# An output projection by seven products of halves, with its weight sums and some attention work made ready early through DRAM

## The chip, the cores and the metric

The kernel runs on one core of a Trainium2 chip. The metric is the time of one launch on the device in microseconds (us), as the median of several runs. The engines named below are TensorE (PE in the profile; PEld is its loading of weights), VectorE (DVE), ScalarE (ACT), GpSimd (POOL) and SyncE (SP), whose queue carries nearly all transfers between DRAM and the on-chip memory.

## The reference

One layer of a hybrid encoder on 1024 prompt frames and 32 single-frame samples, all in float32, D_MODEL = 1024:

```python
h = rmsnorm(x, g_mix)
proj = h @ w_in
q, k, v, cb, cc, cx, ga, gc = jnp.split(proj, SPLITS, axis=-1)
...
y_attn = attend(q, k, v).reshape(b, t, SB_WIDTH) @ w_attn_out
conv_out, new_buf = causal_conv(cc * cx, conv_buf, conv_w)
y_conv = (cb * conv_out) @ w_conv_out
merged = jax.nn.sigmoid(ga) * y_attn + jax.nn.sigmoid(gc) * y_conv
x = x + merged @ w_o
f = jnp.square(jax.nn.relu(rmsnorm(x, g_ffn) @ w_up)) @ w_down
x = x + f
x = x + jax.nn.sigmoid(rmsnorm(x, g_ple) @ w_ple_gate) * (p @ w_ple)
```

`attend` is a strictly causal stick-breaking attention with 8 heads of 64. The change concerns `merged @ w_o`, a product of 1024 x 1024 weights with 1056 columns, and the work that feeds `merged`.

## The kernel before, in words

All 1056 columns (prompt and samples) are handled at once, features on the 128 partitions, so a 1024-feature matrix is 8 blocks of 128 x 1056. Each float32 operand is split into a high part (rounded to the fp32r form by a cast on ACT, `whi`, `mh`) and a low part (the rest, a subtraction on DVE, `wlo`, `ml`); each product is three matmuls: high x high, high weight x low, low weight x high.

The stages follow each other on PE: the first gate groups, the input projection in 18 column sets, the start of the attention, the attention, the two branch projections (`branches`), the output projection (`output_projection`), the MLP's up and down projections, and the gated embedding. The input, up and down projections already use seven products of halves instead of eight (`seven`): with the weights in quadrants A11, A12, A21, A22 and the columns in halves, sums S1 to S4 of weight quadrants and T1 to T4 of operand quadrants are formed, and the products A11·B11, A12·B21, A22·T4, S1·T1, S2·T2, S3·T3, S4·B22 give the result.

The output projection before is the plain product: `wo_group` makes, for each of 8 output blocks and each third of the columns (352), 8 x 3 matmuls; `wo_post` adds the group to x in DRAM order, `wo_high` and `wo_low` split the weights one block ahead, `wo_after` squares the new x and makes the MLP's operands of it, `wo_sums` their T1 to T4, which go out to DRAM and come back for `up_early`, the first products of the MLP.

What sets the order: on PE, ACT, DVE and POOL the instructions run in the order in which the program text issues them (`tc.manual_schedule`), each engine in order, and an instruction that has to wait holds all that stand behind it on its engine. Small generators in the list `side` are stepped once per group of matmuls and so lay the preparation of the next weights between the groups; in the attention a planned list of filler matmuls (`plan_gates`, `plan_rest`) stands between the steps. The transfers stand on SP's queue in one order, which a scheduler fixed when the kernel was built; a transfer that waits for its data holds those behind it too. Buffers come in rings: 34 blocks of 128 x 1056 (`blk`), 4 raw weight blocks, and 2 buffers each for the split weights `whi` and `wlo`. A new tile waits until the last reader of the one that had the buffer is done.

The gate rows (16 blocks of 128 x 1056, eight for the attention branch, numbers 0 to 7, and eight for the convolution, 8 to 15) are made in the input projection, kept in DRAM (`gd`), and read again in `branch_fetch`; `branch_scale` and `branch_sigmoid` finish them on DVE and ACT before `branch_post` multiplies.

## Time and profile before

| what | value |
|---|---|
| time of the runs shown | median 1539.77 us (1539.54 to 1540.97, 3 runs) |
| the profiled execution | 1540.83 us, with a span of 1539.1 us |
| granted TensorE clock in it | 0.998 |
| PE busy over the span | 1517.4 us (99%) |
| DVE, ACT, POOL busy | 1082.9, 751.3, 294.9 us |
| input projection in the span | 63.6 to 391 us |
| start and body of the attention | 391 to 401.6 and 401.6 to 602.6 us |
| branch projections | 602.6 to 672.8 us |
| output projection | 672.8 to 766.1 us |
| first products of the MLP (`up_early`) | 766.1 to 791.5 us |
| down projection | 1098 to 1426.2 us |

The bounds of the stages were read from the first and last matmul of each stage's groups. Tables by stretch give, for each stretch, its length and each engine's busy time with its count of instructions in brackets. A group of instructions is given by its line in the kernel, its engine, the names of output and inputs without buffer numbers, and the shape; matmuls of one stream overlap, so that the distance between their starts, not the mean duration, is their cost. In a list of waits, "A <- B" is an instruction A that waited for B. Of a stretch in time order, each row has the start, the duration and, in brackets, the engine's idle time before it and what ended it.

### The profile page before, as it was taken

What the parts mean: (1) busy time and instruction counts of PE and PEld (TensorE: products, weight loads), DVE (VectorE), ACT (ScalarE), POOL (GpSimd) and SP (SyncE); (2) the same over time, 40 slices, a digit from 0 to 9 for tenths busy, and PEclk for the clock granted to TensorE, in tenths of its full rate; (3) what the DMA queues carried; (4) which work ended last, traced back from release to release, by engine and by line L of the source; (5) the groups of instructions that cost most, each with busy time, mean ns of one, the idle gap of its engine ahead of it and who ended that gap; (6) DMA issues with size and microseconds to landing.
All of it is one profiled execution on the core that took longest, in us unless ns stands there. A gap on an engine that the chain in (4) does not pass through costs nothing.

```text
span 1539.1 us, 29455 instructions
## 1 busy us (share of the span) xinstructions
PE 1517.4 (99%) x11792; PEld 1505.0 (98%) x11792; DVE 1082.9 (70%) x1483; ACT 751.3 (49%) x1378; POOL 294.9 (19%) x324
## 2 busy tenths in 40 slices
...
GB/s 217 205 52 114 192 153 193 167 43 129 240 126 242 223 124 123 147 167 182 128 199 171 160 175 169 149 138 154 304 283 200 280 334 236 203 274 121 138 129 117
DMA packets 112009, 273.21 MB, mean 178 GB/s; under 512 B 13152, under 2 KB 30304, under 8 KB 111872
## 3 DMA queue, kind: packets, MB, share of 16 engines
...
q14 instruction: 45, 0.37, 0.1%
...
## 4 chain that ended last, share of the span: by engine, by line
PE 62%; ACT 1%; DVE 1%; DMA 0%; issue 0%; DVEq 0%
PE ps_dn L1759 7%; PE ps_dn L1758 7%; PE ps_dn L1757 7%; PE ps_A11u L242 3%; PE ps_A11u L241 3%; PE ps_A11u L240 3%; PE ps_pg L118 2%; PE ps_S1u L241 2%; PE ps_S1u L240 2%; PE ps_wo L1433 2%; PE ps_wo L1432 2%; PE ps_wo L1431 2%; PE ps_S1u L242 2%; PE ps_pg L120 2%; PE ps_pg L119 2%; PE ps_oa L118 1%
## 5 line engine op out<-in xcount | busy, mean ns | idle before, releaser
L1759 PE MATMUL ps_dn<-fh,wlo_dn 128*128 128x264 f32 x896 | 255.2, 285 | 0.0
L1758 PE MATMUL ps_dn<-fl,whi_dn 128*128 128x264 f32 x896 | 254.9, 284 | 0.0
L1757 PE MATMUL ps_dn<-fh,whi_dn 128*128 128x264 f32 x896 | 254.7, 284 | 0.0
L1759 PEld LDWEIGHTS ps_dn<-fh,wlo_dn 128*128 128x128 f32 x896 | 168.6, 188 | 0.1
L1757 PEld LDWEIGHTS ps_dn<-fh,whi_dn 128*128 128x128 f32 x896 | 168.7, 188 | 0.0
L1758 PEld LDWEIGHTS ps_dn<-fl,whi_dn 128*128 128x128 f32 x896 | 168.5, 188 | 0.0
L207 POOL TENSOR_TENSOR s_i<-raw_i,raw_i 128x512 f32<-128x512 f32 x32 | 44.2, 1381 | 240.0 <-DVE slS_i L168 209.9
L852 DVE TENSOR_TENSOR_SCAN r<-r 128x128 f32<-128x128 f32 (+3 forms) x64 | 86.4, 1349 | 3.4 <-POOL r L845 3.4
L1644 ACT CAST whi_dn<-raw_dn 128x1024 fp32r<-128x1024 f32 x40 | 42.0, 1050 | 82.8 <-PE ps_dn L1758 82.6
L1650 DVE TENSOR_TENSOR wlo_dn<-raw_dn,whi_dn 128x1024 fp32r<-128x1024 f32 x40 | 61.2, 1530 | 28.6 <-ACT whi_dn L1644 28.6
L240 PE MATMUL ps_A11i<-T,shS_i 128*128 128x264 f32 x256 | 73.1, 285 | 0.0
L242 PE MATMUL ps_A11i<-T,slS_i 128*128 128x264 f32 x256 | 72.9, 285 | 0.0
L241 PE MATMUL ps_A11i<-T,shS_i 128*128 128x264 f32 x256 | 72.7, 284 | 0.0
L207 POOL TENSOR_TENSOR s_u<-raw_u,raw_u 128x512 f32<-128x512 f32 x22 | 32.1, 1459 | 210.3 <-DVE slS_u L168 126.8
L892 DVE TENSOR_TENSOR at<-pa,at 128x512 fp32r<-128x512 f32 (+2 forms) x96 | 51.9, 550 | 26.6 <-ACT at L891 22.1
L1670 DVE TENSOR_TENSOR fl<-mr,fh 128x1056 fp32r<-128x1056 f32 x56 | 69.9, 1247 | 0.2 <-ACT q L1710 0.2
L168 DVE TENSOR_TENSOR slS_i<-s_i,shS_i 128x512 fp32r<-128x512 f32 x48 | 35.0, 734 | 49.6 <-ACT shS_i L166 49.4
L1519 ACT ACTIVATE m<-m 128x528 f32<-128x528 f32 (+1 forms) x52 | 31.7, 610 | 73.2 <-DVE m L287 28.3
L845 POOL TENSOR_SCALAR_AFFINE_SELECT r<-r 128x128 f32<-128x128 f32 x64 | 30.5, 477 | 187.1 <-ACT r L838 175.8
L1841 POOL TENSOR_TENSOR xx<-xx,pgs 128x384 f32<-128x384 f32 (+1 forms) x23 | 24.3, 1058 | 217.0 <-DVE pgs L1840 210.4
L1433 PE MATMUL ps_wo<-mh,wlo_wo 128*128 128x352 f32 x192 | 62.1, 324 | 0.0
L1432 PE MATMUL ps_wo<-ml,whi_wo 128*128 128x352 f32 x192 | 62.1, 323 | 0.0
...
## 6 DMA issues: line engine op xcount, KB each, us to landing
raw_dn<-in_w_down_dram SPq DMA_DIRECT2D x56, 512.0 KB, 4.6
raw_i<-in_w_in_dram SPq DMA_DIRECT2D x36, 512.0 KB, 4.5
mr<-mdT SPq DMA_DIRECT2D x32, 528.0 KB, 5.6
raw_u<-in_w_up_dram SPq DMA_DIRECT2D x32, 512.0 KB, 3.6
mr<-mdB SPq DMA_DIRECT2D x24, 528.0 KB, 6.0
...
raw_pg<-in_w_ple_gate_dram SPq DMA_DIRECT2D x17, 512.0 KB, 3.5
...
```

What stands on the lines that cost most here:

```text
L207: f()
L240: nc.tensor.matmul(p_, wh[:, k, :], o[:, 0, c], start=new and n == 0, stop=False, **on)
L241: nc.tensor.matmul(p_, wh[:, k, :], o[:, 1, c], start=False, stop=False, **on)
L242: nc.tensor.matmul(p_, wl[:, k, :], o[:, 0, c], start=False, stop=z, **on)
L852: nc.vector.tensor_tensor_scan(rev, rev, rev, 1.0, ALU.mult, ALU.bypass)
L1432: nc.tensor.matmul(ps, hi[:, k, :], ml[k][:, c], start=False, stop=False, skip_group_check=True)
L1433: nc.tensor.matmul(ps, lo[:, k, :], mh[k][:, c], start=False, stop=k == KD - 1, skip_group_check=True)
L1650: dve(lo, raw, hi.bitcast(F32), op=sub)
L1670: dve(l, mraw.pop(v), opd[v].bitcast(F32), op=sub)
L1757: nc.tensor.matmul(ps, hi[:, j, :], oh, start=j == 0, stop=False)
L1758: nc.tensor.matmul(ps, hi[:, j, :], ol, start=False, stop=False)
L1759: nc.tensor.matmul(ps, lo[:, j, :], oh, start=False, stop=j == NP_ - 1)
```

## The change

`w_o` is multiplied by seven products. The 28 products of 128 output rows (4 row pairs j, 7 kinds) each run over two quarters of 264 columns, 4 blocks of weights and 3 matmuls, 672 matmuls of 264 columns in place of 576 of 352: first the four A12·B21, then per row pair A11, A22 (of the pair before), S1, S2, S4, S3, and last A22 of pair 3. Each product is added to x, held in quadrants, as soon as it is done (`dve` lines in `output_projection`), and each quadrant goes to DRAM by itself.

The weight sums S1 to S4 are made in 16 pieces (`ahead_wo`) while the input projection's sets 6 onward run, split into high and low, and kept in DRAM (`wsd`); 8 pieces split `w_attn_out` in the same way (`ahead_attn`, kept in `aod`) in the first 48 steps of the attention, and four gate rows, 4 to 7, are scaled and put through the sigmoid (`ahead_gate`, kept in `gs_`) in the last two sets of the input projection and the start of the attention. So that these four exist by then, the first two sets compute rows 4 to 7, and rows 0 to 3 are made by the planned filler in place of 4 to 7. In `branches` the attention products read the split weights, and rows 4 to 7 ready to use. The operands B11, B21, B22 and T1 to T4 of the new product (`wop`) are made from `merged` in the branches and in the projection's first groups. The MLP's operands B21 and B22 of row pairs 0 to 2 are made after the projection from x read back from DRAM (`xg`, `xh`), and B11 late in it.

In the diff, lines with "..." stand for what is left out.

```diff
+AHEAD_AT = {6: 14, 16: 14}
...
-    SETS = [("g", 0), ("g", 2)] + [(nm, 0) for nm in ("cc", "cx", "cb", "q", "k", "v")] + [("g", 8)]
+    SETS = [("g", 4), ("g", 6)] + [(nm, 0) for nm in ("cc", "cx", "cb", "q", "k", "v")] + [("g", 8)]
...
+    def ahead_wo(j, k):
+
+        t = blk(f"wr{j}{k}", F32R, [P, 2, 2, 2, P])
+        raw = t[:, 1].bitcast(F32)
+        for i in range(2):
+            nc.sync.dma_start(raw[:, i], w_o[2 * j + i][:, 2 * k : 2 * k + 2, :])
+        for _ in range(3):
+            yield
+        a11, a12, a21, a22 = raw[:, 0, 0], raw[:, 0, 1], raw[:, 1, 0], raw[:, 1, 1]
+        dve(a22, a21, a22, op=add)
+        dve(a21, a11, a21, op=sub)
+        dve(a11, a22, a11, op=sub)
+        dve(a12, a11, a12, op=sub)
+        nc.scalar.copy(t[:, 0], raw)
+        yield
+        dve(t[:, 1], raw, t[:, 0].bitcast(F32), op=sub)
+        nc.sync.dma_start(wsd[j][:, :, :, k, :].rearrange("x s p n -> p (x s) n"), t.bitcast(F32).rearrange("p x r e n -> p (x r e) n"))
+        yield
+
+    def ahead_attn(n):
+        t = blk(f"ao{n}", F32R, [P, 2, 4, P])
+        raw = t[:, 1].bitcast(F32)
+        nc.sync.dma_start(raw, w_attn_out[n])
+        for _ in range(3):
+            yield
+        nc.scalar.copy(t[:, 0], raw)
+        dve(t[:, 1], raw, t[:, 0].bitcast(F32), op=sub)
+        nc.sync.dma_start(aod[n], t.bitcast(F32).rearrange("p e k n -> p e (k n)"))
+        yield
+
+    def ahead_gate(n):
+        m = blk(f"ga{n}")
+        nc.sync.dma_start(m, gd[n])
+        for _ in range(3):
+            yield
+        scaled(m)
+        yield
+        nc.scalar.activation(m, m, AF.Sigmoid)
+        nc.sync.dma_start(gs_[n - 4], m)
+        yield
+
+    AHEAD = [partial(ahead_wo, j, k) for j in range(4) for k in range(4)]
+    AHEAD += [partial(ahead_gate, n) for n in range(4, 8)] + [partial(ahead_attn, n) for n in range(KD)]
+
+    def ahead_some(n):
+        for _ in range(min(n, len(AHEAD))):
+            yield from AHEAD.pop(0)()
...
+            w = wraw.tile([P, 2, 4, P], F32R, tag="raw", name=f"raw_o{nm}{n}")
+            nc.sync.dma_start(w.bitcast(F32).rearrange("p e k n -> p e (k n)"), aod[n])
         sg = blk(f"s{nm}{n}")
-        nc.sync.dma_start(sg, gd[n + (8 if nm == "c" else 0)])
+        nc.sync.dma_start(sg, gd[n + 8] if nm == "c" else gs_[n - 4] if n > 3 else gd[n])
...
+        if nm == "a":
+            made[b] = tuple(fetched[b][0][:, i] for i in range(2))
+            return
...
+    wop = {k: [None] * 4 for k in ("B11", "B21", "B22", "T1", "T2", "T3", "T4")}
+
+    def part_high(k, j, src):
+        d = wop[k][j] = blk(f"o{k}{j}", F32R, [P, 2, TH])
+        nc.scalar.copy(d[:, 0, :], src)
+
+    def part_low(k, j, src):
+        d = wop[k][j]
+        dve(d[:, 1, :], src, d[:, 0, :].bitcast(F32), op=sub)
+        wop[k][j] = d[:, 0, :], d[:, 1, :]
...
+    def merge_sums(n, ks=("T3", "T2", "T4")):
+
+        a, b = halves
+        e, o = mg[n - n % 2], mg[n // 2 * 2 + 1] if n % 2 else None
+        if o is None:
+            dve(e[:, a], e[:, a], e[:, b], op=sub)
+            return
+        for k in ks:
+            if k == "T3":
+                dve(e[:, b], o[:, b], e[:, b], op=sub)
+            elif k == "T2":
+                dve(o[:, b], o[:, b], e[:, a], op=add)
+            else:
+                dve(o[:, a], o[:, a], o[:, b], op=sub)
...
+    def turn_part(k, j):
+
+        n, c = 2 * j + (k in ("T2", "T4")), halves[k in ("T2", "T3")]
+        part_high(k, j, mg[n][:, c])
+        part_low(k, j, mg[n][:, c])
...
+                proj_high("A12", 1)
+                proj_low("A12", 1)
+                proj_fetch("A12", 2)
...
+            elif s_ in AHEAD_AT:
+                prior = ahead_some(AHEAD_AT[s_])
+                side.append(prior)
...
+            if n < 48:
+                next(prior, None)
...
+    PROJ = [("A12", "B21", j) for j in range(4)]
+    for j in range(4):
+        PROJ += [("A11", "B11", j)] + [("A22", "T4", j - 1)] * (j > 0)
+        PROJ += [("S1", "T1", j), ("S2", "T2", j), ("S4", "B22", j), ("S3", "T3", j)]
+    PROJ += [("A22", "T4", 3)]
+    AT = {(k, j): 2 * i for i, (k, _, j) in enumerate(PROJ)}
...
+    def proj_fetch(k, j):
+        if k in PLACE:
+            r, e = PLACE[k]
+            oraw[k, j] = wraw.tile([P, 4, P], F32, tag="raw", name=f"raw_{k}o{j}")
+            nc.sync.dma_start(oraw[k, j], w_o[2 * j + r][:, e::2, :])
+            return
+        ow[k, j] = w = [fpool.tile([P, 4, P], F32R, tag=g, name=f"{g}o{k}{j}", bufs=SHB) for g in ("sh", "sl")]
+        for i in range(2):
+            nc.sync.dma_start(
+                w[i].bitcast(F32).rearrange("p k n -> p (k n)"), wsd[j, i, PART[k]].rearrange("p k n -> p (k n)")
+            )
...
+        for q, k in enumerate(("S1", "S2", "S4", "S3")):
+            at(q, proj_fetch, k, 0)
+        for j in (2, 3):
+            at(2 * j - 3, proj_high, "A12", j)
+            at(2 * j - 2, proj_low, "A12", j)
+        at(2, xload, "ce", 2)
+        at(2, xload, "ce", 3)
+        at(3, xload, "xb", 0)
+        at(3, xload, "m2", 0)
+        at(1, merge_high, last, "2")
+        for q, k, j in (
+            (1, "T1", 0), (2, "T1", 1), (3, "T1", 2), (4, "T1", 3), (6, "T2", 0), (7, "T2", 1), (8, "T2", 2), (9, "T2", 3),
+            (10, "T3", 0), (11, "T3", 1), (12, "T3", 2), (13, "T3", 3), (14, "T4", 0), (15, "T4", 1), (16, "T4", 2), (17, "T4", 3),
+        ):
+            at(q, turn_part, k, j)
+        at(3, merge_low, last, "2")
+        at(4, merge_sums, last, ("T3",))
+        at(5, merge_sums, last, ("T2",))
+        at(6, merge_sums, last, ("T4",))
+        for (k, j), q in AT.items():
+            if k in ("A11", "A22"):
+                at(max(1, q - 9), proj_fetch, k, j)
+                at(q - (3 if (k, j) == ("A11", 0) else 5), proj_high, k, j)
+                at(q - (2 if (k, j) == ("A11", 0) else 4), proj_low, k, j)
+            elif k != "A12" and j:
+                at(q - 6, proj_fetch, k, j)
...
+        def again(j):
+            if j % 2 == 0:
+                x21[0] = blk(f"xg{j}", F32, [P, 2, TH])
+            x21[j + 1] = x21[0][:, j % 2, :]
+            nc.sync.dma_start(x21[j + 1], xd[2 * j + 1][:, halves[0]])
...
+        for j in range(3):
+            at(AT["S4", 3] + 2 + j // 2, again, j)
+        at(end - 12, early_up, 0)
+        at(end - 10, early_up, 1)
+        at(end - 4, early_split, "u0")
+        at(end - 2, early_split, "u1")
+        at(end - 1, second, 0)
...
+            for t in range(2):
+                on = (z if k in ("S1", "S4") else x).get((j, t)) if k not in ("A11", "S1") else None
+                if i < 2:
+                    proj(k, b, j, t, on, range(3, 4), False, True)
+                else:
+                    p_ = proj(k, b, j, t, on)
+                    (z if k in ("S1", "S4") else x)[j, t] = p_
+                for f in jobs.pop(2 * i + t, ()):
+                    f()
...
+                if k in ("A11", "A12"):
+                    dve(x11, p_, x11, op=add)
+                elif k == "S1":
+                    dve(x22, x22, p_, op=sub)
+                elif k == "S2":
+                    dve(x12, p_, x12, op=add)
+                elif k == "S4":
+                    dve(x12, x12, p_, op=sub)
+                elif k == "S3":
+                    dve(x22, p_, x22, op=add)
+                else:
+                    dve(x21_, p_, x21_, op=add)
...
+        up_operand("B21", 3, x1[3][2])
+        keep_x(3, 2)
+        for j in (1, 2):
+            second(j)
+        square_x(3, 2)
+        up_operand("B22", 3, x1[3][3])
+        add_square(last)
...
+                    elif i == 2 and j < 3:
+                        if j % 2 == 0:
+                            pair = blk(f"xh{j}", F32, [P, 2, TH])
+                        x22[j] = pair[:, j % 2, :]
+                        nc.sync.dma_start(x22[j], xd[2 * j + 1][:, halves[1]])```

Three places where instructions now stand otherwise. Each row is one instruction (or several alike, x2) with its line, its operation, output and inputs, and shape; the names are the program's with the index left out, and a number tells buffers apart.

The first is SP's queue at the start of the attention. `q` are the first queries, `ks` and `vv` keys and values, `ga` a gate row, `gs_` its place in DRAM, `m_i` results of the last input set, `cv` cached values. Before:

```order
L808 DMA vv_4855<-vd 128x1024
L820 DMA q_4945<-qd 64x2x256
L821 DMA q_4945<-qd 64x256
L822 DMA q_4945<-qd 64x256
L820 DMA q_4949<-qd 64x2x256
L821 DMA q_4949<-qd 64x256
L822 DMA q_4949<-qd 64x256
L1280 DMA gd<-m_i_4612 128x1056
L1280 DMA gd<-m_i_4613 128x1056
L820 DMA q_4955<-qd 64x2x256
```

and with the change:

```order
L860 DMA vv_5035<-vd 128x1024
L651 DMA ao_5110<-in_w_attn_out_dram 128x512
L872 DMA q_5130<-qd 64x2x256
L873 DMA q_5130<-qd 64x256
L667 DMA gs__158<-ga_5001 128x1056
L874 DMA q_5130<-qd 64x256
L872 DMA q_5134<-qd 64x2x256
L873 DMA q_5134<-qd 64x256
L874 DMA q_5134<-qd 64x256
L1384 DMA gd<-m_i_4778 128x1056
L1384 DMA gd<-m_i_4779 128x1056
L872 DMA q_5140<-qd 64x2x256
```

The last of the four finished gate rows (the last `gs_` row) now stands between the second and the third load of the first `q`; before, the queue went from one `q` load to the next.

The second is ACT at the start of the output projection. `w0oA` is the high part of a weight quadrant (the third and fourth A12, then the first A11), `raw_A` the same as loaded; `oB` and `oT` are operands of the new product, `mg` and `sc` blocks of `merged`. Before, `whi_wo` is the high part of a weight block and `mh` that of `merged`:

```order
L971 ACTIVATE sa_8456<-sa_8456 128x1056
L1417 CAST whi_wo_8572<-raw_wo_8512 128x1024
L991 CAST mh_8589<-mg_8183 128x1056
L991 CAST mh_8610<-mg_8293 128x352 x2
L1417 CAST whi_wo_8635<-raw_wo_8569 128x1024
L991 CAST mh_8610<-mg_8293 128x352
L1417 CAST whi_wo_8725<-raw_wo_8632 128x1024
```

With the change:

```order
L1551 CAST w0oA_8805<-raw_A12o_8763 128x512
L1052 CAST oB_8826<-mg_8506 128x528
L1551 CAST w0oA_8889<-raw_A12o_8809 128x512
L1052 CAST oB_8891<-mg_8506 128x528
L1052 CAST oT_8893<-sc_6064 128x528
L1052 CAST oT_8911<-sc_7001 128x528
L1551 CAST w0oA_8922<-raw_A12o_8874 128x512
L1052 CAST oT_8928<-mg_8192 128x528
L1052 CAST oT_8948<-mg_8395 128x528
L1551 CAST w0oA_8967<-raw_A11o_8896 128x512
```

The casts of the first T operands (`oT` from `sc`) stand behind the cast of the third A12.

The third is DVE at the same place: `w1oA` is the low part of a weight quadrant, `ceo` the x quadrant to which a product in `ps_wo` is added. Before, the low parts of the weights and the three additions of block 0:

```order
L994 TENSOR_TENSOR ml_8611<-mg_8293,mh_8610 128x352
L1423 TENSOR_TENSOR wlo_wo_8707<-raw_wo_8569,whi_wo_8635 128x1024
L1436 TENSOR_TENSOR xr_8511<-ps_wo_0_8638,xr_8511 128x352
L1436 TENSOR_TENSOR xr_8511<-ps_wo_1_8660,xr_8511 128x352
L1436 TENSOR_TENSOR xr_8511<-ps_wo_2_8682,xr_8511 128x352
L1423 TENSOR_TENSOR wlo_wo_8752<-raw_wo_8632,whi_wo_8725 128x1024
```

With the change:

```order
L1693 TENSOR_TENSOR ceo_8786<-ps_woA_8829,ceo_8786 128x264
L1056 TENSOR_TENSOR oT_8893<-sc_6064,oT_8893 128x528
L1693 TENSOR_TENSOR ceo_8786<-ps_woA_8839,ceo_8786 128x264
L1555 TENSOR_TENSOR w1oA_8906<-raw_A12o_8809,w0oA_8889 128x512
L1056 TENSOR_TENSOR oT_8911<-sc_7001,oT_8911 128x528
L1693 TENSOR_TENSOR ceo_8786<-ps_woA_8849,ceo_8786 128x264
L1056 TENSOR_TENSOR oT_8928<-mg_8192,oT_8928 128x528
L1056 TENSOR_TENSOR oB_8891<-mg_8506,oB_8891 128x528
L1693 TENSOR_TENSOR ceo_8786<-ps_woA_8859,ceo_8786 128x264
L1555 TENSOR_TENSOR w1oA_8946<-raw_A12o_8874,w0oA_8922 128x512
L1056 TENSOR_TENSOR oT_8948<-mg_8395,oT_8948 128x528
L1080 TENSOR_TENSOR mg_8395<-mg_8506,mg_8395 128x528
```

Between the additions of the first groups stand the low parts of T1 and of the weights, and the sums that make T3, T2 and T4 of the last pair.

286 lines of the change are left out of this document (172 added, 114 removed).

## The prediction

> **What bounds the kernel now.** The page's head first: PE is busy nearly all of the span, no other engine is.
>
> ```profile
> span 1539.1 us, 29455 instructions
> PE 1517.4 (99%) x11792; PEld 1505.0 (98%) x11792; DVE 1082.9 (70%) x1483; ACT 751.3 (49%) x1378; POOL 294.9 (19%) x324
> ```
>
> So a change pays only through what PE has to do and through what PE waits for. The table by stretch shows where that is: in order the input projection, the start of the attention, the attention, the branches, the output projection, the MLP's first products, and the down projection for comparison.
>
> ```profile
> core 0: us, PE busy (x) PEld busy (x) DVE busy (x) ACT busy (x) POOL busy (x), PEclk, DMA share, GB/s
> 63.60:391.00 327.40, 326.59 (x2669) 325.34 (x2668) 216.17 (x292) 146.33 (x315) 93.73 (x60) 1.00 0.40 138
> 391.00:401.60 10.60, 10.60 (x89) 10.60 (x88) 3.69 (x5) 3.34 (x7) 0.00 (x0) 1.00 0.56 168
> 401.60:602.60 201.00, 198.05 (x1531) 189.91 (x1530) 167.11 (x236) 124.64 (x282) 40.31 (x130) 1.00 0.58 175
> 602.60:672.80 70.20, 69.65 (x434) 69.36 (x434) 55.37 (x75) 26.96 (x32) 0.00 (x0) 1.00 0.48 158
> 672.80:766.10 93.30, 93.30 (x580) 93.30 (x579) 44.38 (x60) 24.81 (x31) 15.24 (x6) 1.00 0.44 158
> 766.10:791.50 25.40, 23.76 (x192) 23.34 (x192) 21.36 (x30) 20.83 (x41) 0.00 (x0) 1.00 0.79 265
> 1098.00:1426.20 328.20, 328.20 (x2691) 328.14 (x2690) 263.53 (x315) 135.78 (x167) 27.62 (x16) 1.00 0.73 244
> ```
>
> The output projection has no idle PE at all, and DVE and ACT are half free in it. The attention is the stretch with the least room on DVE (167 of 201), and `up_early` the one where DVE and ACT are both over 80% busy. The list of PE's waits says the same: of waits in the stretches that the change touches there are only these of any size, two of them in `up_early` (1.6 + 0.7 = 2.3 us).
>
> ```profile
> PE ps_eu L240 <- ACT pe L221: 1.6, 1, 1.6
> PE av L909 <- DVE at L892: 1.2, 2, 0.7
> PE ps_A11u L242 <- DVE wlo_u L110: 0.7, 1, 0.7
> ```
>
> **The gain: fewer matmul columns.** The distance between matmuls is read from the first and the last start of a product's groups, for the plain product (352 columns) and for the down projection, which already has the form that the change brings (264 columns).
>
> ```profile
> L1431 PE MATMUL ps_wo<-mh,whi_wo x192: 318/323/328, 673.0 to 765.6; 128*128 128x352 f32 x192
> L1433 PE MATMUL ps_wo<-mh,wlo_wo x192: 317/323/328, 673.3 to 765.9; 128*128 128x352 f32 x192
> ...
> L1757 PE MATMUL ps_dn<-fh,whi_dn x896: 278/284/291, 1098.1 to 1425.8; 128*128 128x264 f32 x180
> L1759 PE MATMUL ps_dn<-fh,wlo_dn x896: 278/284/373, 1098.4 to 1426.1; 128*128 128x264 f32 x180
> ```
>
> 576 matmuls from 673.0 to 765.9 are 92.9 / 575 = 161.6 ns each (161.9 with the whole stretch, 93.3 / 576); 2688 from 1098.1 to 1426.1 are 328.0 / 2687 = 122.1 ns. So the projection goes from 93.2 us to 672 x 122.1 ns = 82.0 us: **-11.2 us** as long as nothing makes PE wait. The other stages keep their counts of matmuls (the gate rows only change places).
>
> The distance per column is the same in both, 0.46 ns; 39.5 ns more for 88 columns leaves about 3 ns that is fixed. [...]
>
> **The cost at the projection's start.** The new product needs much small preparation in its first groups, in the fixed order of ACT and DVE. Its pieces, by rows of the same shapes:
>
> ```profile
> L168 DVE TENSOR_TENSOR slA_i<-raw_i,shA_i 128x512 fp32r<-128x512 f32 x16 | 11.0, 689 | 20.9 <-ACT shA_i L166 20.9
> L287 DVE TENSOR_TENSOR m_i<-ps_A12i,p_i 128x264 f32<-128x264 f32 x32 | 13.1, 425 | 6.4 <-PE ps_A12i L242 6.4
> L166 ACT CAST shA_i<-raw_i 128x512 fp32r<-128x512 f32 x16 | 10.0, 623 | 0.1
> ```
>
> Back to back they follow each other some 0.1 us faster than they last, as the T operands in `up_early` show (three in 1.94 us on DVE; two ACT starts 0.53 apart):
>
> ```profile
> 774.51 1.94 DVE L162 TENSOR_TENSOR T<-rt,T 128x528 fp32r<-128x528 f32 x3
> ...
> 776.33 0.64 ACT L161 CAST T<-w 128x528 fp32r<-128x528 f32 x1
> 776.86 0.65 ACT L1558 ACTIVATE ce<-ce 128x528 f32<-128x528 f32 x1
> ```
>
> So I take 0.62 us for a 528-column subtraction or sum, 0.60 for a 512-column one, 0.35 for adding a 264-column product, 0.53 and 0.62 for the casts. Count from the first matmul. The first two A12 take three of their four blocks in both quarters, 36 matmuls, then the last block, 3 matmuls a group. The third A12's cast needs the buffer of the first A12 (two buffers), free after 42 matmuls, at 5.15 us. ACT then runs that cast, B22_3 and T1_0: 5.15 + 0.62 + 0.53 + 0.63 = 6.9. DVE has added the first group at about 5.2 and stands at the low part of T1_0 until 6.9; behind it queue that low part, the second group's addition and the low part of the third A12: 6.9 + 0.62 + 0.35 + 0.60 = 8.5. PE's third matmul of the third A12 wants it at 50 x 0.122 = 6.1: a stall of 2.4 us. From there DVE does not rest. Up to the fourth A12's low part it has 3 pieces of 0.62, 2 additions and 0.60: 8.5 + 3.2 = 11.7, wanted 24 matmuls (2.9 us) after 8.5 = 11.4, a stall of 0.2. Up to the first A11's low part it has 5 of 0.62, 2 of 0.35 and 0.60 more: 16.0, wanted at 14.6, a stall of 1.4. After that the parts are ahead of PE: the T2 parts are wanted only six groups later. Sum **+4.0 us**. If DVE's order did not matter, the buffer alone would cost 5.15 + 0.62 + 0.60 = 6.4 against 6.1, 0.3 us; if each of the pieces took its full duration, about 5.5. I take 4.0, since each step is in an order that can't change.
>
> The rest of the projection has transfers for it: half-sized weight sums come back from DRAM in high and low parts.
>
> ```profile
> DMA packets 4818, 14.74 MB, mean 158 GB/s; under 512 B 544, under 2 KB 544, under 8 KB 4813
> ```
>
> That is the projection before. After, S1 to S4 bring 16 x 512 KB = 8.4 MB, a quarter of the 4.2 MB of w_o falls away, x read again adds 0.8 MB: some 22.9 MB in 86 us, 266 GB/s, as much as `up_early` moves now (265). Hidden, taken at 0.
>
> **The cost at the attention's start.** The last finished gate row's store now stands on SP between the loads of the first queries. The rows before, ACT, SP, PE and transfers in turn:
>
> ```profile
> 400.39 0.38 ACT L706 COPY sg<-ps_g 128x264 f32<-128x264 f32 x1 [1.62 <-PE ps_g L704]
> ...
> L621 ACT ACTIVATE m_i<-m_i 128x1056 f32<-128x1056 f32 x6 | 6.6, 1092 | 0.0
> ...
> 395.12 0.60 SPq L821 DMA_DIRECT2D q<-qd  x1
> 395.76 0.59 SPq L822 DMA_DIRECT2D q<-qd  x1
> ...
> 401.70 0.28 PE L835 MATMUL z<-ks,q 128*128 128x128 f32 x1
> ...
> q<-qd SPq DMA_DIRECT2D x3, 128.0 KB, 3.0
> q<-qd SPq DMA_DIRECT2D x5, 64.0 KB, 3.4
> ```
>
> Before, the third load was issued at 395.76, 6 us ahead of the matmul at 401.70 that reads it. With the change it stands behind the store, and the store waits for the row's sigmoid, which stands on ACT behind the second copy of the filler gate (the row at 400.39, tied to PE). The sigmoid starts at 400.7 and ends at 401.8, the store's issue takes 0.6, the load lands 3.4 us after its issue began: 401.8 + 0.6 + 3.4 = 405.8. The second matmul of the first scores needs it, and PE is in order: 405.8 - 401.7 = 4.1. With the 3.0 us of the larger ones it would be 3.7; I take **+3.9**. The next queries' loads stand behind it with 0.6 us each, about as late as their readers: no more. PE has no idle time in that stretch to pay from.
>
> **The smaller terms.** *After the projection*: `up_early` gets five more operand pairs (B21 and B22 of the pairs 0 to 2, less one that falls into the projection), and one weight split less.
>
> ```profile
> L1373 DVE SCALAR_TENSOR_TENSOR B<-xr,vecT,B 128x528 fp32r<-128x528 f32 x12 | 8.8, 761 | 0.0
> L110 DVE TENSOR_TENSOR wlo_u<-raw_u,whi_u 128x1024 fp32r<-128x1024 f32 x12 | 15.2, 1263 | 3.8 <-ACT whi_u L109 2.9 <-DMA raw_u<-in_w_up_dram 0.9
> ```
>
> 5 x 0.76 - 1.26 = 2.5 us more on DVE, which has 25.4 - 21.4 = 4.0 free: between -1.6 (the first wait goes, since both first weights are split earlier) and +2.5. I take +0.6. *Input projection*: 16 pieces with four additions of 128 x 128 columns, a cast and a low part each, some 1.5 us of DVE, 24 us over a stage in which DVE has 111 us free; PE feels it only where one of them waits for a transfer and an addition that PE needs stands behind. 0 to +8 (the rival below); I take +0.5. *Attention*: 8 pieces of 0.60 on DVE and 0.52 on ACT, 4.8 us of the 34 that DVE has free: 0 to +4.8, taken +0.5. *Branches*: DVE loses eight low parts of 512 and four scalings and gains sums and more, smaller parts; 15 us free there, and PE idles 0.5: 0, between -0.5 and +1.
>
> **Sum**: -11.2 + 4.0 + 3.9 + 0.6 + 0.5 + 0.5 = **-1.7 us**. The sum belongs to the profiled execution, 1540.83 us (span 1539.1 and 1.7 around it), which is 1.06 above the median of the runs. Against that median of 1539.77 I predict **1538.1 us**. This kernel's measurement can tell 0.2%, 3.1 us, from no change.
>
> **The rivals.**
> *Only one of the two stalls is there* (a load that lands sooner, an ACT order that the waits treat more kindly): -1.7 - 4 = -5.7, 1534.1 us. For it: each stall is a chain of four or five steps worked out by hand. Against: each engine is in order and the waits are between named instructions.
> *Neither*, PE alone counts: -11.2 + 1 = -10, 1529.6 us. For it: the down projection, same form, has PE busy 328.20 of 328.20 us. Against: that stage's weights are prepared by a long, even stream, not from a standing start.
> *The attention pays its pieces in full*: DVE is its busiest helper, and the pieces go in the steps where scans and the attention weights share it. -0.5 + 4.8 added: +2.6, 1542.4 us. Against: fillers on PE between the steps.
> *Slower*: in the input projection, DVE stands at a piece whose load or store has not landed, with the addition of a product behind it. The nearest rows for such a transfer are:
>
> ```profile
> raw_i<-in_w_in_dram SPq DMA_DIRECT2D x36, 512.0 KB, 4.5
> mr<-mdT SPq DMA_DIRECT2D x32, 528.0 KB, 5.6
> ```
>
> PE goes on without an addition for about three groups of 12 matmuls, 4.4 us; a wait of 5.6 costs 1.2 us. If half of the 16 pieces hit one, +9.6 instead of +0.5: net +7.4, 1547.2 us. It decides from about five such pieces on (net over 3.1). For it: 28 of 34 blocks are in use there, so pieces take turns with the results' blocks. Against: a piece's load is issued three steps ahead.
> *The weight load paces*, 161.9 ns for each matmul however many columns: 108.8 us for the projection, net +25, 1565 us. Only the down projection's rows speak, and against it. [...]
>
> **How the numbers follow.** Forecast 0.55, within it 0.15 of the weight below -3.1 us; one stall 0.17; neither 0.05; attention in full 0.09; slower 0.13; weight load 0.01. Faster by over 0.2% then is 0.15 + 0.17 + 0.05 = 0.37, slower 0.14, no change 0.40 + 0.09 = 0.49. The forecast alone spans 1535 to 1542. The range, 1532 to 1543.5, takes in the one-stall case and the attention case and leaves out the two ends.
>
> **What would show it.** 672 matmuls 122 ns apart from the tenth group on; PE waits of about 2.4, 0.2 and 1.4 us for low parts of A12 and A11 in the first 16 us; one PE wait of about 4 us for a `q` transfer at the first scores; no PE wait over 1 us in the input projection. Wrong it is if the first or second of these stalls is missing (faster), or if the input projection is more than 3 us longer than 327.4 (slower).

## The result and the profile after

The changed kernel takes **1595.51 us** (median of 4 runs, 1594.4 to 1598.03), the kernel before beside it 1539.94 (1539.54 to 1540.97): a ratio of 1.0362, 95% interval 1.0344 to 1.038. It is 3.6% slower; predicted were 1538.1 us and no change.

The head of the profiled execution's page shows that PE has not only waited, it has also been busy for longer (before: 1517.4 us):

```profile
span 1594.9 us, 30094 instructions
PE 1527.8 (96%) x11888; PEld 1508.4 (95%) x11888; DVE 1147.5 (72%) x1633; ACT 762.7 (48%) x1424; POOL 301.4 (19%) x324
```

To see where, both spans are cut at the same matmuls: from the last first-gate product to the end of the input projection's sets (input), to the second matmul of the first scores (z), to the first attention output product (attention), to the first output projection product (branches), to the end of `up_early` (projection and up_early), to the first down product (up), and the rest. The table by stretch of the changed kernel, first five stages (length, each engine's busy time with its count, the granted clock, the DMA share and GB/s):

```profile
core 0: us, PE busy (x) PEld busy (x) DVE busy (x) ACT busy (x) POOL busy (x), PEclk, DMA share, GB/s
57.60:437.40 379.80, 349.43 (x2744) 343.43 (x2742) 260.57 (x378) 158.99 (x343) 95.28 (x60) 0.96 0.48 162
437.40:452.50 15.10, 9.80 (x64) 9.21 (x62) 5.50 (x6) 5.13 (x9) 0.00 (x0) 0.86 0.73 206
452.50:666.40 213.90, 207.20 (x1565) 197.92 (x1566) 175.90 (x250) 131.01 (x293) 45.88 (x130) 0.99 0.66 208
666.40:730.50 64.10, 64.10 (x398) 64.10 (x397) 47.73 (x72) 13.55 (x19) 0.00 (x0) 1.00 0.49 165
730.50:847.00 116.50, 108.66 (x864) 107.10 (x864) 82.68 (x142) 52.60 (x95) 14.82 (x6) 0.99 0.79 263
```

and the same stretches of the kernel before:

```profile
57.50:394.20 336.70, 335.87 (x2743) 334.41 (x2742) 220.96 (x299) 152.58 (x327) 93.73 (x60) 1.00 0.40 140
394.20:401.70 7.50, 7.50 (x64) 7.50 (x63) 1.23 (x1) 2.09 (x4) 0.00 (x0) 1.00 0.49 165
401.70:609.40 207.70, 204.21 (x1568) 195.78 (x1568) 171.85 (x243) 126.87 (x286) 40.31 (x130) 1.00 0.58 177
673.00:791.60 118.60, 116.96 (x769) 116.54 (x769) 65.77 (x91) 45.54 (x72) 15.24 (x6) 1.00 0.52 180
```

Of the 55.8 us that the span grew, the input projection has 43.1 (379.8 - 336.7), the start of the attention 7.6, the attention 6.2, the branches 0.5; the two stages for which the change was made gain 2.1, and the rest is within 0.5. In the input projection PE stood for 30.4 us (379.80 - 349.43; before 0.8), and was busy 13.6 us longer (349.43 - 335.87) with the same matmuls, at a granted clock of 0.96.

The list of PE's waits, in the same order as the page gives them:

```profile
PE ps_A11i L241 <- DVE m_i L295: 17.4, 7, 7.9
PE ps_A11i L241 <- ACT u_i L285: 6.5, 5, 3.6
...
PE ps_woA L1728 <- DVE w1oA L1555: 3.4, 2, 2.2
PE pt_v L572 <- DVE dv L559: 3.4, 1, 3.4
PE z L887 <- DMA q<-qd: 2.9, 1, 2.9
PE ps_eu L243 <- DVE wlo_eu L111: 2.5, 2, 1.7
PE ps_g L754 <- ACT m_i L746: 2.0, 1, 2.0
PE ps_eu L241 <- ACT pe L222: 1.9, 2, 1.7
```

The first, second and fourth rows are the input projection: `m_i` and `u_i` are the additions and copies that empty the products' accumulators, on DVE and ACT. The waits for `w1oA` and `q` were forecast; those for `wlo_eu` and `pe` lie in `up_early`, for which the forecast had +0.6 us in all. What DVE and ACT stood for in that stage:

```profile
DVE m_i L288 <- DMA wsd<-wr: 8.9, 2, 4.7
DVE wr L638 <- DMA wr<-in_w_o_dram: 8.6, 3, 4.1
DVE m_i L295 <- DMA kd<-m_i: 4.4, 1, 4.4
...
ACT wr L642 <- DVE wr L641: 69.3, 13, 15.3
```

`wr` is the block in which a piece of weight sums is made, `wsd` its place in DRAM. DVE waits for the landing of a piece's store (the next result `m_i` takes the block from which it is stored), for the landing of a piece's load, and for the landing of a result's store. ACT's cast of a piece (L642) waits for DVE's sums, and holds the copies behind it. ACT itself stood at two transfers of pieces too, 7.9 us at a load and 4.5 us at a store.

How one such wait grows is seen in the longest of them, in order of time (start, duration, engine, line; in brackets the idle time before and what ended it; SPq are transfers as they are issued):

```profile
181.28 0.69 DVE L644 TENSOR_TENSOR wr<-wr 128x512 fp32r<-128x512 f32 x1
182.00 0.37 SPq L645 DMA_DIRECT2D wsd<-wr  x1
186.17 0.77 DVE L288 TENSOR_TENSOR m_i<-ps_A12i,p_i 128x264 f32<-128x264 f32 x2 [4.20 <-DMA wsd<-wr]
186.86 1.21 DVE L548 TENSOR_TENSOR m_i<-m_i,kh 128x1024 fp32r<-128x1024 f32 x1
188.10 0.81 SPq L634 DMA_DIRECT2D wr<-in_w_o_dram  x2
188.96 5.42 SPq L549 DMA_DIRECT2D kd<-m_i  x2
192.46 0.43 DVE L295 TENSOR_TENSOR m_i<-ps_A11i,s_i 128x264 f32<-128x264 f32 x1 [4.39 <-DMA kd<-m_i]
192.95 0.59 PE L241 MATMUL ps_A11i<-T,shA_i 128*128 128x264 f32 x1 [7.87 <-DVE m_i L295]
```

A piece is stored at 182.00. The next addition needs its block and starts only at 186.17, when the store has landed. Through that the low part of a key block (L548) is late, and its store stands on SP behind the loads of the next piece (188.10). The addition after that needs this block, and waits a second time, 4.39 us. Two waits of 4.3 us in a row leave PE 7.87 us without work.

And then PE starts at half the clock. PEclk, the granted clock, is 1.00 or 0.50 throughout this trace. It is 0.50 (half speed below) from 188.71, 222.84, 267.22 and 407.16 us in the input projection, from 441.30 and 451.54 in the next two stages, from 816.76 in `up_early`, and again from 1588.18 to the end. These starts are 10, 13, 41, 10, 3, 107 and 226 steps of 3.41 us apart, and the stretches before the last are one to three such steps long. The table by stretch, cut into these steps:

```profile
188.71:198.95 10.24, 6.00 (x27) 6.00 (x28) 6.00 (x13) 2.25 (x5) 0.65 (x1) 0.50 0.52 174
222.84:226.25 3.41, 3.09 (x15) 3.12 (x16) 1.95 (x7) 1.56 (x4) 0.00 (x0) 0.50 0.11 45
260.39:263.80 3.41, 1.68 (x14) 1.46 (x12) 2.48 (x6) 1.45 (x2) 0.00 (x0) 1.00 0.00 0
267.22:270.63 3.41, 3.41 (x16) 3.18 (x16) 2.63 (x4) 0.18 (x1) 0.00 (x0) 0.50 1.03 369
274.04:277.46 3.42, 1.73 (x12) 1.52 (x12) 2.93 (x8) 1.73 (x4) 0.00 (x0) 1.00 0.85 303
407.16:417.40 10.24, 6.59 (x28) 6.29 (x29) 7.13 (x15) 1.66 (x3) 0.00 (x0) 0.50 0.48 156
437.88:441.30 3.42, 1.68 (x12) 1.62 (x13) 2.90 (x4) 1.97 (x4) 0.00 (x0) 1.00 1.03 311
441.30:444.71 3.41, 3.41 (x18) 3.41 (x17) 1.26 (x1) 0.53 (x2) 0.00 (x0) 0.50 1.01 229
468.60:472.02 3.42, 1.68 (x14) 1.43 (x13) 1.22 (x2) 1.87 (x4) 0.37 (x1) 1.00 0.77 241
734.84:738.25 3.41, 2.10 (x16) 1.77 (x15) 1.29 (x4) 2.49 (x5) 0.00 (x0) 1.00 0.92 317
738.25:741.67 3.42, 2.49 (x20) 2.49 (x21) 3.42 (x8) 1.32 (x3) 0.00 (x0) 1.00 0.37 117
813.35:816.76 3.41, 1.70 (x13) 1.49 (x13) 3.20 (x3) 0.18 (x1) 1.44 (x1) 1.00 0.49 190
```

From 441.30 to 444.71 PE is busy all the time, and its matmuls start 0.22 us apart, 16 of them from 441.31 to 444.60 (3.29 / 15), where 28 at a distance of 122 ns would fit. The four rows at half speed in the input projection have 86 matmuls (those cut by the ends of a row with them) in 19.09 us of busy PE, 222 ns each. At 122 ns they would take 10.5 us: by this estimate 8.6 of the 13.6 us by which PE was busy longer are half speed, and the other 5.0 are not explained here.

The length of one wait does not tell whether half speed follows. In the steps before 441.30 and 816.76 waits of 1.96 and 1.71 us end, and PE was busy for 1.68 and 1.70 us of these steps. The wait of 2.24 us that ends at 739.18 lies across two steps, with 2.10 and 2.49 us busy, and nothing followed. Counted over this trace, between 60 and 1500 us: half speed came after each of the five full-speed steps with PE busy for 1.51 us or less, after two of the five with 1.68 to 1.73 us (not after those at 260.39, 274.04 and 468.60), and after none of the 399 with 1.92 us or more. What decides among the five is not shown.

### The profile page after: what moved, and what is told of

Same layout as the page of the kernel before. It is cut to its first block, busy times and chain, and to the rows that moved or that the text cites. A ratio compares the mean times of both kernels' runs of the same rounds, so it can differ in the third digit from the quotient of the medians.

```text
span 1594.9 us, 30094 instructions
## 1 busy us (share of the span) xinstructions
PE 1527.8 (96%) x11888; PEld 1508.4 (95%) x11888; DVE 1147.5 (72%) x1633; ACT 762.7 (48%) x1424; POOL 301.4 (19%) x324
## 3 DMA queue, kind: packets, MB, share of 16 engines
q8 instruction: 93, 1.52, 0.4%
## 4 chain that ended last, share of the span: by engine, by line
PE 58%; DVE 2%; ACT 1%; DMA 1%; issue 1%; DVEq 0%; ACTq 0%; SPq 0%
PE ps_dn L2001 7%; PE ps_dn L2002 7%; PE ps_dn L2000 7%; PE ps_A11u L242 3%; PE ps_A11u L243 3%; PE ps_A11u L241 3%; PE ps_woA L1728 3%; PE ps_pg L119 2%; PE ps_S1u L242 2%; PE ps_S1u L241 2%; PE ps_S1u L243 2%; PE ps_pg L120 2%; PE ps_pg L121 2%; PE ps_woS L1728 1%; PE ps_oa L121 1%; PE ps_oa L119 1%
## 5 line engine op out<-in xcount | busy, mean ns | idle before, releaser
L241 PE MATMUL ps_A11i<-T,shS_i 128*128 128x264 f32 x256 | 74.9, 293 | 7.0 <-ACT u_i L285 6.5
L897 POOL TENSOR_SCALAR_AFFINE_SELECT r<-r 128x128 f32<-128x128 f32 x64 | 36.1, 565 | 206.8 <-ACT r L890 195.7
L243 PE MATMUL ps_A11i<-T,slS_i 128*128 128x264 f32 x256 | 73.5, 287 | 0.0
L169 DVE TENSOR_TENSOR slS_i<-s_i,shS_i 128x512 fp32r<-128x512 f32 x48 | 40.9, 857 | 35.0 <-ACT shS_i L167 33.3
L169 DVE TENSOR_TENSOR slS_u<-s_u,shS_u 128x512 fp32r<-128x512 f32 x48 | 35.4, 738 | 35.2 <-ACT shS_u L167 35.2
L1908 ACT CAST fh<-mr 128x1056 fp32r<-128x1056 f32 x56 | 60.0, 1074 | 0.0
```

The costliest lines, as they stand in the source:

```text
L169: dve(l, src, h.bitcast(F32), op=sub)
L241: nc.tensor.matmul(p_, wh[:, k, :], o[:, 0, c], start=new and n == 0, stop=False, **on)
L243: nc.tensor.matmul(p_, wl[:, k, :], o[:, 0, c], start=False, stop=z, **on)
```

## The experiments

Each total is one run unless an interval is given. Stages are cut as above, in us of the profiled execution; the kernel before took 1539.9 to 1543.3 us beside them. The expectations of e1, e3 and e4 count the input projection from a bound 6.0 us later (373.8 us in the change, 330.7 before). In e1, e9 and e11 the projection reads split attention weights in place of the weight sums, and e3 stores values that are not the sums: they time the work, not the result.

| run | total | input | z | attention | branches | projection + `up_early` |
|---|---|---|---|---|---|---|
| before | 1539.94 | 336.7 | 7.5 | 207.7 | 63.6 | 118.6 |
| after | 1595.51 | 379.8 | 15.1 | 213.9 | 64.1 | 116.5 |
| e1_none | 1554.29 | 344.7 | 12.2 | 211.0 | 64.0 | 115.5 |
| e3_nomath | 1570.3 | 357.5 | 12.9 | 213.4 | 63.5 | 116.0 |
| e4_spread | 1610.89 | 395.4 | 13.0 | 214.8 | 64.0 | 115.9 |
| e5_gates | 1592.58 | 376.5 | 11.7 | 217.0 | 64.0 | 116.4 |
| e7_own | 1632.16 | 419.9 | 11.8 | 213.1 | 64.1 | 116.5 |
| e7_ownslow | 1593.73 | 379.2 | 13.5 | 212.3 | 63.9 | 116.5 |
| e9_work | 1593.49 | 380.1 | 11.9 | 214.3 | 63.6 | 116.6 |
| e9_dma | 1586.37 | 372.6 | 11.4 | 214.9 | 64.1 | 116.4 |
| e11_rings | 1573.34 | 363.3 | 12.5 | 211.0 | 64.1 | 115.7 |
| e11_work | 1574.4 | 359.7 | 14.1 | 213.7 | 63.7 | 116.0 |
| e8_inplace | 1555.85 | 337.0 | 7.4 | 207.3 | 63.6 | 133.0 |
| e10_early | 1542.74 | 337.3 | 7.5 | 207.1 | 64.6 | 120.0 |
| e13_squares | 1592.71 | 380.9 | 12.7 | 213.7 | 64.1 | 113.8 |
| e12_tuned | 1540.91 | 337.4 | 7.5 | 208.0 | 64.6 | 117.5 |
| e12_again | 1539.27 | 337.4 | 7.5 | 207.2 | 64.6 | 114.4 |
| e14_tuned | 1537.45 | 337.6 | 7.8 | 208.7 | 64.6 | 112.3 |

### e1: no weight sums in the input projection

```diff
-AHEAD_AT = {6: 14, 16: 14}
+AHEAD_AT = {16: 12}
-    AHEAD = [partial(ahead_wo, j, k) for j in range(4) for k in range(4)]
-    AHEAD += [partial(ahead_gate, n) for n in range(4, 8)] + [partial(ahead_attn, n) for n in range(KD)]
+    AHEAD = [partial(ahead_gate, n) for n in range(4, 8)] + [partial(ahead_attn, n) for n in range(KD)]
```

> The 16 pieces that make the weight sums in the input projection are left out; the projection reads split attention weights from DRAM in their place, equally many and equally long transfers, so its numbers are meaningless, its instructions the same. The gate rows' work then starts at once in set 16. If the pieces are what lengthens the input projection (373.8 us, before 330.7), it returns to 330 to 333 us and the time falls to 1546 to 1553 us. If the swapped gate rows or the transfers of another part were the cause, it stays above 360 us and the time above 1580.

1554.29 us, 41 less than the change. The input projection takes 344.7 (338.7 in the count of the expectation, more than the 330 to 333 there): the 16 pieces cost 35.1 of its 43.1 us. The other 8.0 belong to the four gate rows and the new order; the gates alone make a wait of the same kind:

```profile
DVE m_i L288 <- DMA gs__158<-ga: 4.9, 1, 4.9
```

### e3: the pieces without DVE's work

```diff
-        dve(a22, a21, a22, op=add)
-        dve(a21, a11, a21, op=sub)
-        dve(a11, a22, a11, op=sub)
-        dve(a12, a11, a12, op=sub)
...
-        dve(t[:, 1], raw, t[:, 0].bitcast(F32), op=sub)
```

> The pieces keep their loads, their block, the cast on ACT and the store, but lose their four sums and the low part on DVE (the stored values are not the weight sums). Theory 'ring': a piece's block belongs to the ring of 34 that also holds the results, and DVE stands for the landing of a store before it may write a result into that block. Then the waits of DVE for landings stay, and the input projection takes 350 to 375 us. Rival 'work': DVE has too much to do. Then it falls to 330 to 337 us, since 24 us of DVE work are gone.

The input projection takes 357.5: without DVE's arithmetic 22.3 of the 35.1 us go, and 12.8 stay for loads, blocks, cast and store. So neither 'ring' nor 'work' has it all. Where DVE no longer stands at the load, ACT does, with its cast:

```profile
ACT wr L638 <- DMA wr<-in_w_o_dram: 30.9, 6, 8.9
```

### e4: one piece to a set, sets 2 to 15

```diff
-AHEAD_AT = {6: 14, 16: 14}
+AHEAD_AT = {16: 28}
...
+            if 2 <= s_ < 16:
+                side.append(after(1, ahead_some(1)))
```

> The same pieces with all their work, but 14 of them spread one to a set over sets 2 to 15 rather than one after the other from set 6 on; the last two, the gates and the attention weights as in the change. By 'ring' the blocks are short only a part of the time: input projection 331 to 350 us, time 1552 to 1573 us. By 'work', and by a rival that blames the 16 MB of transfers, the same work and bytes cost about the same: 360 us or more, 1582 us or more.

Slower: 395.4 us, 15.6 more than the change. Giving the pieces more room between them does not help, against the theory 'ring' as it was put. In the waits of DVE the store of the piece itself is on top:

```profile
DVE m_i L288 <- DMA wsd<-wr: 14.8, 3, 5.0
DVE m_i L295 <- DMA wsd<-wr: 11.0, 4, 5.0
```

Seven results, in place of two, took the block of a piece whose store had just been issued. Which result meets which block depends on how often the ring of 34 blocks is drawn on; one piece to a set seems to put the two in step, which no run shows by itself.

### e5: the gate rows earlier

```diff
-    AHEAD += [partial(ahead_gate, n) for n in range(4, 8)] + [partial(ahead_attn, n) for n in range(KD)]
+    AHEAD[14:14] = [partial(ahead_gate, n) for n in range(4, 8)]
+    AHEAD += [partial(ahead_attn, n) for n in range(KD)]
```

> As the change, but the four gate rows are finished ahead of the last two weight pieces, so that no gate row's store stands between the first queries' loads. If that store is what held the first scores, PE's wait of 2.9 us for the query transfer goes and the stretch from the input projection's end to the second score's matmul falls from 15.0 us to 8 to 11; the time falls by 2 to 6 us, if the two weight pieces that now lie in the attention cost nothing. If the wait only moves to another transfer, the stretch stays at 13 us or more.

The start of the attention falls from 15.1 to 11.7 us, where 8 to 11 were expected, and what PE and its weight loads stand for `q` at `z` falls from 6.4 us (3 waits) to 2.8 (2 waits), so that the gate row's store between the loads caused the larger part of it. The two weight pieces that now come after the gates stand in the attention, which takes 3.1 more.

### e7: a block of its own for the pieces

```diff
-        t = blk(f"wr{j}{k}", F32R, [P, 2, 2, 2, P])
+        t = wpool[0].tile([P, 2, 2, 2, P], F32R, tag="W", name=f"wr{j}{k}", bufs=1)
...
-        h = wpool[0].tile([P, 4, P], F32R, tag="sh", name=f"sh{name}", bufs=SHB)
+        h = wpool[0].tile([P, 4, P], F32R, tag="sh", name=f"sh{name}", bufs=SHB if inproj[0] else 3)
```

(and the low parts `sl` likewise; this gives the memory for the block). In e7_ownslow the sums also come five steps after the load, in place of three.

> As the change, but a weight piece has a buffer of its own (one, 4 KB a partition; the input projection's rings of split half weights go from 4 to 3 buffers each to make room), so that it takes no block of the ring of 34. Theory 'ring': no result of DVE in the input projection waits for a piece's store any more; with one buffer the pieces wait for each other, so DVE still waits for their loads. The list of DVE's waits then shows no result waiting for the store into the weight sums' place; the stage (379.8 us in the change, 336.7 before, by the last first-gate matmul) takes 350 to 375 us. Rival 'work': the ring has no part, 375 us or more.

> As the run before, with five groups instead of three between a piece's load and its sums. Theory: with neither the ring nor the load to stand for, DVE keeps only the pieces' work, and the stage takes 338 to 350 us, the time 1555 to 1568. Rival 'work': 370 us or more, as the work is the same. A third, that three buffers for the split half weights are too few: waits of PE for those low parts in the list.

419.9 and 379.2 us: no gain, where 350 to 375 and 338 to 350 were expected. The waits for `wsd` are gone from DVE's list, and the load has their place, since with one block it can't begin before the store of the piece before has landed. In e7_own:

```profile
DVE wr L639 <- DMA wr<-in_w_o_dram: 42.7, 12, 6.1
ACT wr L643 <- DVE wr L642: 96.8, 16, 11.6
```

In e7_ownslow the first row is 18.6 us. So a transfer can be stood for at either end. But the runs changed two things, and the next ones showed that the second matters.

### e9 and e11: the work alone, the transfers alone, and the control

e9_work does the arithmetic of the 16 pieces on one block that is loaded once; e9_dma loads and stores without arithmetic; both with the block and rings of e7. e11_rings is e1 with the rings of e7, no piece at all. e11_work is e9_work with every ring as in the change and a 128 x 128 tile, on which instructions of the same kinds run:

```diff
-        t = blk(f"wr{j}{k}", F32R, [P, 2, 2, 2, P])
-        for i in range(2):
-            nc.sync.dma_start(raw[:, i], w_o[2 * j + i][:, 2 * k : 2 * k + 2, :])
+        w = one[0]
+        raw = w.bitcast(F32)
...
+        dve(raw, raw, raw, op=add)
+        dve(raw, raw, raw, op=sub)
+        dve(raw, raw, raw, op=add)
+        dve(raw, raw, raw, op=sub)
+        for _ in range(2):
+            nc.scalar.copy(w, raw)
...
+        for _ in range(2):
+            dve(w, raw, raw, op=sub)
```

(One cast and one low part of 512 columns are here two of 128 each. The busy time in the stage is that of the change all the same: 260.97 us of DVE and 158.57 of ACT, where the change has 260.57 and 158.99.)

> The pieces' arithmetic alone: the four sums, the cast and the low part are done 16 times in the same places on one private buffer that is loaded once; no piece loads or stores anything else (the split attention weights stand in for the weight sums in the projection, so the numbers are meaningless). One weight-ring size is 3 for 4, as in the private-buffer runs. If what PE pays in the input projection is the work itself on DVE and ACT, the stage stays at 365 us or more (the change: 379.8; without pieces 344.7). If it is the standing for transfers in the engines' order, it falls to 345 to 352 us.

> The pieces' transfers alone: each loads its weights into a private buffer and stores them twice to DRAM, as many bytes as in the change, with nothing on DVE or ACT (the projection reads the split attention weights instead). If transfers and SP's queue by themselves hold up the stage, 360 us or more; if only the engines' standing for them does, 344 to 350 us. With both this and the run beside it near 345, neither the work nor the traffic but their coupling costs the 35 us.

> A control for the private-buffer runs: no pieces at all, as in the first run that left them out (stage 344.7 us), but with 3 for 4 buffers in the input projection's rings of split half weights. If the smaller rings cost nothing, 344 to 347 us, and the private-buffer runs can be read as they stand. If they do (a run with the pieces' transfers alone had no work and still took 372.6), 360 us or more, and those four runs tell of the rings, not of the pieces.

> The pieces' arithmetic alone with all rings as in the change: in the place of each piece DVE does four sums of 128 x 128 and two low parts of 128 columns, ACT two casts, some 1.8 and 0.5 us, all on one small private block; no loads, no stores, no block of the ring (the split attention weights stand in for the weight sums). If the work is what PE pays for, 365 us or more; if the standing for transfers is, 345 to 350 us.

The control takes 363.3 us: rings of 3 in place of 4 cost 18.6 us by themselves (363.3 - 344.7), and e7 and e9 are to be read against it. Then transfers alone cost 9.3, work alone 16.8, both 15.9 where the sums come late enough, and 56.6 where they stand at the load. With the rings of the change, work alone costs 15.0 (359.7 - 344.7), and transfers with the cast 12.8 (e3). Together they cost 35.1, more than the sum; on the smaller rings the whole, 15.9, was less than the sum of the parts, so such differences are not shares.

So about 15 us are lost without any transfer, by work that has room in the sum of DVE's time. The list of waits of e11_work shows through whom:

```profile
PE ps_A11i L241 <- ACT u_i L285: 6.6, 5, 2.4
PE ps_A11i L241 <- DVE m_i L295: 5.1, 5, 2.9
...
ACT wr L645 <- DVE wr L643: 62.2, 15, 7.5
```

15 times ACT stands at a piece's cast until DVE has come to the sums, for 4.1 us each (62.2 / 15). Where copies `u_i` stand behind it, they are late, and PE with them; elsewhere it is an addition of DVE itself that is late. The longest of the waits for a copy, in order of time:

```profile
249.73 0.63 ACT L645 CAST wr<-wr 128x128 fp32r<-128x128 f32 x2 [5.70 <-DVE wr L643]
252.66 0.38 ACT L285 COPY u_i<-ps_A11i 128x264 f32<-128x264 f32 x1
253.09 0.39 PE L241 MATMUL ps_A11i<-T,shS_i 128*128 128x264 f32 x1 [2.43 <-ACT u_i L285]
```

From 245.01 to 248.52 DVE scaled two results (L531), and the piece's sums stood behind that.

### e8: nothing made early

The other question is what the seven products give by themselves. e8 has the gates, the attention weights and the sets as before, and POOL makes the weight sums inside the projection, a row pair at a time:

```diff
+    def pair_sums(j):
+        r1, r2 = pair_raw.pop(j)
+        a11, a12, a21, a22 = r1[:, 0::2, :], r1[:, 1::2, :], r2[:, 0::2, :], r2[:, 1::2, :]
...
+        pool(s3, a11, a21, op=sub)
+        pool(a21, a21, a22, op=add)
+        pool(s2, a21, a11, op=sub)
+        pool(s4, s2, a12, op=sub)
```

> The seven products without anything made early: no pieces in the input projection, gate rows and attention weights as before the change; the weight sums are formed in the projection by the otherwise idle fourth engine (POOL) from w_o as it is loaded, as the input projection does it, split there on ACT and DVE, and the second to fourth A12 get buffers of the other ring, so that no cast waits for the first A12's. Theory: all stages up to the output projection as before (first matmul of it at 673 to 674 us), the output projection with the MLP's first products in 109 to 115 us where it took 118.6, the whole 1531 to 1537 us. Rival: DVE, slowed by POOL's sums, holds PE up by more than the 11 us gained, 1541 us or more.

The input projection, the attention's start, the attention and the branches return to 337.0, 7.4, 207.3 and 63.6 us, those of before: the branches didn't need what was made early. But projection and `up_early` take 133.0, with POOL busy for 40.14 us and a clock of 0.94:

```profile
672.20:805.20 133.00, 115.42 (x864) 111.93 (x864) 112.28 (x163) 62.95 (x115) 40.14 (x22) 0.94 0.60 198
```

Beside POOL, DVE took longer for the same work. In e8 the low part of an operand (L995, 128x528) takes 0.69 us at 692.48, with POOL idle from 690 to 696, and 1.76 us at 686.35, with POOL busy for 3.40 of the 6 us from 684 to 690. The change itself shows it, with POOL adding the squares of the new x:

```profile
813.16 2.71 DVE L111 TENSOR_TENSOR wlo_eu<-raw_eu,whi_eu 128x1024 fp32r<-128x1024 f32 x1 [1.65 <-ACT whi_eu L110]
818.20 1.23 DVE L111 TENSOR_TENSOR wlo_eu<-raw_eu,whi_eu 128x1024 fp32r<-128x1024 f32 x1 [1.65 <-ACT whi_eu L110]
...
812.33 2.46 POOL L1587 TENSOR_TENSOR ssq<-ssq,sq 128x1056 f32<-128x1056 f32 x1 [6.07 <-ACT sq L1583]
815.92 0.39 PE L243 MATMUL ps_eu<-B,wlo_eu 128*128 128x264 f32 x1 [1.71 <-DVE wlo_eu L111]
```

The same subtraction takes 1.23 us at 818.20, with POOL idle, and 2.71 beside POOL's addition. That addition ends at 812.33 + 2.46 = 814.79, and the subtraction at 813.16 + 2.71 = 815.87, 1.08 us later. What holds DVE up in this time is not shown.

### e13: the change, with its last two squares added by DVE, after `up_early`

```diff
-    sqs = {}
+    sqs, LATE_SQ = {}, (6, 7)
...
-            (dve if n == KD - 1 else pool)(ssq1, ssq1, sqs.pop(n), op=add)
+            (dve if n in LATE_SQ else pool)(ssq1, ssq1, sqs.pop(n), op=add)
...
-        add_square(last)
...
+        for n in LATE_SQ:
+            add_square(n)
```

> The change, with one thing moved: the squares of the last two rows are added by DVE after the MLP's first products instead of one of them by POOL while the first of their weights is split. In the change that split took 2.71 us instead of 1.22 beside POOL's addition, PE waited 1.7 us for it and then ran at half speed for some 4 us. If POOL's sharing is the cause, that split takes 1.2 us, the wait falls to 0.5 us or less, no slow matmuls follow, and the two stages take 111 to 114 us (116.5 in the change). If the order of ACT and DVE alone is the cause, 115 us or more.

Projection and `up_early` fall from 116.5 to 113.8, and PE's waits for `wlo_eu` from 2.5 to 1.0. The longest of these waits is 0.7 us, before 1.7. The granted clock of the stretch is 1.00, where the change has 0.99, so that no half speed follows: POOL's addition beside the subtraction was what made this wait long.

### e10, e12 and e14: the sums on DVE, and their order

e10 is e8 with the sums on DVE, spread over the groups, one more square added by DVE, and six of the T parts made in the branches:

```diff
-        pool(s3, a11, a21, op=sub)
-        pool(a21, a21, a22, op=add)
-        pool(s2, a21, a11, op=sub)
-        pool(s4, s2, a12, op=sub)
+        dve(s3, a11, a21, op=sub)
+        dve(a21, a21, a22, op=add)
+        yield
+        dve(s2, a21, a11, op=sub)
+        yield
+        dve(s4, s2, a12, op=sub)
+        yield
...
+            if ready and len(early) < 6:
+                early.append(ready.pop(0))
+                turn_part(*early[-1])
```

> As the run with the sums formed in the projection (133.0 us for the projection and the MLP's first products), but the sums are DVE's, 0.6 us each, instead of POOL's, six of the T operands are made in the branches, and the last squares are added by DVE, so that POOL and DVE share less time. If DVE's slowing by POOL was what cost 25 us there, the two stages take 110 to 118 us and the whole 1531 to 1540; if DVE simply has too much to do, 122 us or more, and PE idles in the branches as well.

Projection and `up_early`: 120.0 in place of 133.0, between the two expectations. e12 keeps that and moves pieces: four T parts early, the first A11 a step sooner, the last T4 sum seven groups later, the last two squares after `up_early`, the first MLP weights and products sooner.

```diff
-            if ready and len(early) < 6:
+            if ready and i < 13 and len(early) < 4:
...
-        at(6, merge_sums, last, ("T4",))
+        at(13, merge_sums, last, ("T4",))
...
-        at(end - 12, early_up, 0)
+        at(41, early_up, 0)
-        at(end - 4, early_split, "u0")
+        at(47, early_split, "u0")
```

> As the run with nothing made early and DVE's sums (120.0 us for the two stages), with four instead of six T operands made in the branches and none in the last ones, the first A11 split before the sums, the MLP's first weights loaded and split some 9 groups earlier, the last two squares added after them. If the order is what still holds PE up there, 111 to 115 us and the whole 1531 to 1536; if DVE has too much work for the stretch, 118 us or more.

117.5 us, where 111 to 115 were expected, the whole 1540.91 beside 1540.02: equal. Timed again with more runs it stayed so:

> The kernel of e12 once more, timed: by its one look 1540.9 us beside 1540.0 before. If nothing of the seven products' gain survives, a ratio of 1.000 within 0.002; if the one look was unlucky, up to 3 us faster.

1539.27 (10 runs) beside 1541.0 (19 runs), a ratio of 0.9993, interval 0.9983 to 1.0002. e12's first profile had a wait of 2.6 us in `up_early` and others for an addition to x. e14 moves three more things:

```diff
-            (dve if n in LATE_SQ else pool)(ssq1, ssq1, sqs.pop(n), op=add)
+            (dve if n in LATE_SQ or n == 5 else pool)(ssq1, ssq1, sqs.pop(n), op=add)
...
-            at(AT["A11", 3] + 3 + j, lambda j=j: up_operand("B11", j, x1[j][0]))
+            at((45, 47, 50, 53)[j], lambda j=j: up_operand("B11", j, x1[j][0]))
...
-                    if i == 1 and j < 3:
+                    if i == 0 and j < 3:
                         fetch_t(j, 1)
```

> The version of e12 (nothing made early in the input projection; weight sums by DVE inside the output projection; gates and attention weights as before, six T parts in the branches) with three changes of order: the square of the sixth column block is also added by DVE, the B11 operands of the first MLP products stand at later steps, and each group's first x load is issued one step earlier. If the order of DVE, ACT and loads takes what is left of the seven products' gain (e12: output projection and up_early together 117.5, of 118.6 before and 112.0 predicted), the waits of PE at eu (2.8) and woS (1.9) shrink and the two stages take 113 to 116 us, the whole 1534 to 1538. If DVE's own work for the weight sums takes it, the two stages stay at 117 us or more and the whole at 1539 to 1542.

(By its code this kernel makes four T parts in the branches, as e12, not six, and what it loads a step sooner are operands T3 and T4.)

**1537.45 us** (10 runs) beside 1541.0: a ratio of 0.9975, interval 0.9966 to 0.9985. It leaves nothing of the reference's work out and beats the kernel before by 0.25%, a small gain but clear of the noise, and the changed one by some 58 us. Projection and `up_early` take 112.3 us; e12 had 117.5 and 114.4 in its two profiles. So order, and one more square moved from POOL to DVE, had held at least a part of what was left. The longest wait of PE that remains there is 1.0 us, for the low part of a weight sum. 50 us out of the middle of e14's projection, from the table by stretch:

```profile
700.00:750.00 50.00, 50.00 (x411) 49.87 (x410) 49.33 (x81) 20.38 (x35) 10.98 (x4) 1.00 0.61 204
```

DVE is now busy for 49.33 of 50.00 us, so that there is little left to gain by order in that part. Of the 6.3 us gained in these stages the other stages give back 4.2 (input 0.9, z 0.3, attention 1.0, branches 1.0, up and the rest 1.0), single profiles that a few tenths can shift; the medians differ by 3.6.

## Why the prediction was wrong

| step of the prediction | predicted | measured |
|---|---|---|
| distance of the new product's matmuls | 122.1 ns | 50.00 us / 411 = 121.7 ns (e14; the 411 include those cut by the two ends, so 122) |
| stalls at the projection's start | 2.4, 0.2 and 1.4 = 4.0 | 2.2 and 1.2 = 3.4, in e13 too |
| output projection and `up_early` together | 118.6 - 11.2 + 4.0 + 0.6 = 112.0 | 116.5; e13 113.8 |
| first scores waiting for `q` | +3.9 | 2.9 + 0.5 for `q`, in a stage that grew by 7.6 |
| attention | +0.5 (0 to +4.8) | +6.2 |
| branches | 0 | +0.5 |
| input projection | +0.5 (0 to +8) | +43.1 |

**The step that failed is the one on the input projection**: "some 1.5 us of DVE, 24 us over a stage in which DVE has 111 us free; PE feels it only where one of them waits for a transfer and an addition that PE needs stands behind". It was taken as +0.5 us; the stage grew by 43.1, and e1 puts 35.1 of that down to the pieces. Its first half took free time in a sum for slack in an order. e11_work, with no transfer of pieces and as much busy time, already loses 15.0 us: PE waits there 6.6 us for copies on ACT, which stand behind casts that wait for DVE's sums, and 5.1 us for additions of DVE that are late themselves. The work was also more than the 24 us: DVE is busy for 260.57 us in the change and 224.95 in e1, 35.6 more. Free time of DVE is worth nothing to a copy that stands on another engine behind a cast.

**The rival that was called slower had the right mechanism and the wrong price.** It put DVE at a piece whose load or store had not landed, which the list of waits shows, and it named the ring of blocks as the way. It priced such a wait at what is above PE's reserve of 4.4 us, 1.2 us, and with half of the 16 pieces hit at +9.6. DVE had only five such waits for pieces, two for stores of 4.4 us on average and three for loads of 2.9, and ACT two more. But one wait makes the next, as at 181 to 193 us: DVE's lateness delayed a store of results, which stood behind the loads of the next piece on SP, and the next result waited for that one. One store of a piece so cost PE 7.87 us, more than six times the price. Then came what no part of the prediction had: after the wait PE ran at half the clock, which by the estimate above makes 8.6 of the 13.6 us by which its busy time grew in this stage. The forecast had a chance of 0.13 for this side, and a time for it that was 48 us too low.

**The stalls at the start were right**, as a sum worked out instruction by instruction in the order of the engines: 3.4 for 4.0, the second small one missing. They came where the chain had put them: the first ended 8.7 us after the first matmul (739.18 - 730.50; forecast 8.5), the second 16.2 (forecast 16.0). The saving of columns was right too: 122 ns is not the 161.9 of the rival in which the weight load paces. The transfers were hidden as said, 263 GB/s in these stages for a forecast of 266 in the projection.

**`up_early` was mis-sized.** 2.5 us of work into 4.0 us of room was taken as +0.6; PE waited 4.4 us for `wlo_eu` and `pe` (before 1.6 for `pe`) and lost some 1.5 more at half speed, by an estimate from the 16 matmuls that start from 816.77 to 820.06, where 28 at 122 ns would fit. In e13, without POOL's square beside DVE, the two stages take 2.7 us less. (The prediction also counted the 0.7 us wait for `wlo_u` as one of `up_early`; it ends at 792.85, behind that stage, and the sum did not use it.)

**The wait for `q`** was there with nearly its size, and e5 took the larger part of it away by moving the gate rows. Its chain is in the trace: the sigmoid ends at 448.82, the store goes out at 448.84 and the third load of `q` at 449.23. What was missed in that stage are the second wait before it (2.0 us for a copy) and the half speed after both.

**The attention** cost more than the rival of full payment, 6.2 for 4.8. The half speed from 451.54 to 458.37 falls almost wholly in it (PE busy 207.20 against 204.21), and in e1, without weight pieces, it is still 3.3 slower than before. Which part is the order of DVE and which the transfers was not tried.

Not settled is the split of the 35.1 us: work alone gives 15.0, transfers with the cast 12.8, and the 7 between their sum and the whole is put down to their meeting, which no run shows apart. A larger ring, the plain test of the ring's part, was not tried, since the memory is full. e7 and e9 stand on rings that differ from the change's, and say something only against e11_rings.
